# Hybrid DeltaNet and attention block: vector rows loaded on another queue, modulation pieces run in the middle of the groups, gate steps at other places

## The chip, the cores and the metric

The kernel runs on one core of a Trainium2 chip. The metric is the device time of one execution in microseconds. A time of a kernel is the median of its runs; beside it stands one execution taken by the profiler, from which all durations below come.

The engines have short names: PE is the matrix engine (PEld its weight loads), DVE the vector engine, ACT the scalar engine, POOL the general one, SP the engine that issues most of the loads. L12 is line 12 of the kernel. One clock column, PEclk, says at which share of full speed PE was allowed to run in a stretch.

## The reference, cut to what matters

One layer on 512 latent tokens (x) and 256 context tokens (ctx), both of width 2048, all in 32-bit floats:

```python
mod = jax.nn.silu(c) @ w_ada + b_ada            # w_ada: 2048 x 6144
shift, scale, gate = split(mod, 3)              # and the same for c_ctx: mod_c
h  = rms_norm(x,   norm_w) * (1 + scale)   + shift
hc = rms_norm(ctx, norm_w) * (1 + scale_c) + shift_c
... = split(h @ w_in), split(hc @ w_in)         # q, k, v of 8 DeltaNet heads, z, gates, q, k, v, z of attention
# DeltaNet heads: short convolution, normed q and k, decay gates, chunked scan in two directions
# attention heads: normed q and k, rotary positions, softmax over context and latent tokens
y = concat(gdn * silu(z), attn * silu(z_a)) @ w_out
return rms_norm(x + gate * y, final_norm_w)
```

The change touches the way to `h`, `hc` and the first head's projections, and the gates of the DeltaNet heads.

## The kernel before, in words

**Three passes.** Each product with `h` is made of three matmuls: the weights and `h` are split into a high and a low part (`whi_w`, `wlo_w`, `w0h`, `w0l`; `hh` and `hL`/`hC`, with L for the 512 latent and C for the 256 context columns), and high times high, high times low and low times high are added up.

**First stage, head.** SP loads a small table of constants (`cmain`), six blocks of 128 tokens (`xs`, 1 MB each: two of context, four of x), then the vector rows: `vrow` (c, c_ctx, b_ada, norm_w and the DeltaNet norm, as rows of 128) and `crow` (convolution taps) in six small DMAs. For each token block, `turn` squares it on ACT (`junk`) and transposes it on PE (`xt`, L314) into `xts`; `spread` makes the norm factors into a row for all partitions (`rp`, `rb`). After block 1, `vec_columns` transposes the vector rows (`pv`, L268), from which silu(c) (`cs`) comes.

**First stage, modulation.** `ada(g)` computes shift and scale for two of the 16 K tiles of 128: it loads four pieces of `w_ada` (`wada`, 1 MB in two DMAs, L352), multiplies each by `cs` (16 matmuls, L355), copies the sums (`part`, L360), transposes them (`adat`, L364) and adds them up to `md`. It is a generator: with `halves` it stops after its second piece, and always once more between `part` and `adat`. The six 1 MB buffers of the `xs` blocks are those of the pieces too. `make_h` then makes h of these two K tiles: `hf` on DVE (L395), its high part `hhL`/`hhC` on ACT (L397), and the low part on DVE (L403).

**First stage, groups.** A loop over eight groups of two K tiles runs the products of the first head. `project(k)` runs five tiles for K tile k: klat, klat1, qlat, vlat, qlat1, where klat, klat1 and vlat take the context columns as well. `slot` counts the ten tiles of a group, 0 to 9. At the slots in `steps` the loop runs the next part of `ada(g + 1)` after that tile, and after the last of them `make_h(g + 1)`. Where `steps` holds slot 10, which is never reached, the rest is done behind the loop of the group. `gate_sums(g)` (L411 and L413) multiplies `hf` by the 32 gate columns `wg`. `first_weights(k)` loads the weights of K tile k (`wraw_w` 256 KB, `w0r` 64 KB) with three buffers each, and splits them on ACT and POOL (`wlo_w`, L130). In the last group, `gates_in` is run in place of `ada`; its second step transposes the gate sums (`gtp`).

**Order.** In the first stage the code's order is PE's order. On the other engines a scheduler places the instructions, and the DMAs of SP's queue are issued in order; each waits for the DMA eight issues earlier and for its buffer.

**Second stage.** Here rows of projection matmuls are run as filler: `pull(n)` runs filler of n rows, `run(gen, n, ...)` alternates steps of a generator with it. `g1` is the generator of the gates of heads 1 to 7, in three steps: sums along the chunk (`gcp`, L555 and L559); exponentials on ACT up to `egl` (L561 to L566) with `gcum` on DVE (L560); a transpose (`gtr`, L570), with more behind it. `gdn_post_q(1)` is the convolution of q of head 1 (`cacc_q`, DVE L221), and `prep` the head's preparation, whose `tvh` and `pxa` follow.

Of the kernel before, what the change touches and what calls it, by code (L numbers as in the profile page):

```python
# [9 lines left out]
F32R = mybir.dt.float32r  # L10
# [58 lines left out]
def build(tc, a):  # L69
# [18 lines left out]
    NG = KT // 2  # L88
# [7 lines left out]
    def low_tile(m, g, dtype, nm):  # L96
        pool_, n, s = lows[m]
        return pool_.tile([128, 2, n], dtype, tag=f"l{s}{g}", bufs=1, name=f"{nm}{s}{g}")
# [185 lines left out]
    def big(shape, nm):  # L284
        return p0.tile(shape, F32, tag="big", bufs=BIG, name=nm)

    xss = []
    for t in range(6):
        xt_ = big([128, D], f"xs{t}")
        SY.dma_start(xt_, a["ctx"][0, t * 128:(t + 1) * 128] if t < 2 else a["x"][0, (t - 2) * 128:(t - 1) * 128])  # L290
        xss.append(xt_)
    SY.dma_start(vrow[64:80], a["c"].rearrange("b (k p) -> (b k) p", p=128))
    SY.dma_start(vrow[80:96], a["c_ctx"].rearrange("(k p) -> k p", p=128))
    SY.dma_start(vrow[0:48], a["b_ada"].rearrange("b (k p) -> (b k) p", p=128))
    SY.dma_start(vrow[48:64], a["norm_w"].rearrange("b (k p) -> (b k) p", p=128))
    SY.dma_start(vrow[96:97], a["gdn_norm_w"])
    SY.dma_start(crow, a["conv_w"][0].rearrange("j (t p) -> (j t) p", p=128))
    banks = [lambda nm: stile([128, 4, 128], nm, "k"), lambda nm: stile([128, 4, 128], nm, "s"),
             lambda nm: stile([128, 4, 128], nm, "o"), lambda nm: btile([128, 4, 128], nm)]
    ssx = p0.tile([128, 6], F32, name="ssx")  # L300
# [38 lines left out]
    def ada(g, halves=False):  # L339

        n, k0, rows = 2, 2 * g, 4
        md = mds[g] = p0.tile([128, 2, 2, 2], F32, tag="md", bufs=4, name=f"md{g}")

        def vec(v):
            return v[:, k0:k0 + n].unsqueeze(2).to_broadcast([128, n, 2])

        ada_ps = gtile([128, 512], f"ada{g}")
        for j in range(KT // rows):
            wt = big([128, rows, 2, 256], f"wada{g}_{j}")
            for s in range(2):  # L350
                src = w_ada[j * rows * 128:(j + 1) * rows * 128, s * D + k0 * 128:s * D + k0 * 128 + 256]
                SY.dma_start(wt[:, :, s], src.rearrange("(k p) c -> p k c", p=128))  # L352
            for r in range(rows):
                kk = j * rows + r
                T.matmul(ada_ps[32 * r:32 * r + 32], lhsT=cs[:, kk], rhs=wt[:, r].rearrange("p s c -> p (s c)"),  # L355
                         start=kk < 4, stop=kk >= KT - 4, skip_group_check=True)
            if j == 1 and halves:
                yield
        part = p0.tile([128, 512], F32, tag="part", bufs=2, name=f"part{g}")
        V.tensor_copy(part, ada_ps)  # L360
        yield
        tp = gtile([128, 4, 128], f"adat{g}")
        for i in range(4):
            T.transpose(out=tp[:, i], in_=part[:, i * 128:(i + 1) * 128], identity=ident)  # L364
        V.tensor_reduce(out=md.rearrange("p s i m -> p (s i) m"),
                        in_=tp.rearrange("p a (g m) -> p a m g", g=4)[:, :, 0:2], axis=AX.X, op=ALU.add)
        V.tensor_tensor(out=md[:, 0], in0=md[:, 0], in1=vec(vT), op=ALU.add)
        V.tensor_tensor(out=md[:, 1], in0=md[:, 1], in1=vec(b1), op=ALU.add)
        mul(V, md[:, 1], md[:, 1], vec(vT[:, 48:64]))
# [18 lines left out]
    def make_h(p_):  # L388

        md = mds[p_]  # L390
        for i in range(2):
            k = 2 * p_ + i
            hf = hfs[k] = p0.tile([128, NTOK], F32, tag="hf", bufs=3, name=f"hf{k}")
            for m_, t0, t1 in ((0, 0, SEQ), (1, SEQ, NTOK)):
                V.scalar_tensor_tensor(out=hf[:, t0:t1], in0=xts[m_, p_][:, i], scalar=md[:, 1, i, m_:m_ + 1],  # L395
                                       in1=rb[:, t0:t1], op0=ALU.mult, op1=ALU.mult)
                S.activation(hh[m_][:, k], hf[:, t0:t1], AF.Identity, bias=md[:, 0, i, m_:m_ + 1])  # L397
        for m_ in range(2):
            hls[m_, p_] = low_tile(m_, p_, F32R, "h")
        for i in range(2):  # L400
            k = 2 * p_ + i
            for m_, t0, t1 in ((0, 0, SEQ), (1, SEQ, NTOK)):
                V.scalar_tensor_tensor(out=hl(m_, k), in0=hfs[k][:, t0:t1], scalar=md[:, 0, i, m_:m_ + 1],  # L403
                                       in1=hh[m_][:, k], op0=ALU.add, op1=ALU.subtract)
# [34 lines left out]
    def gates_in():  # L439

        V.tensor_copy(gsh, gps[96:128, 0:2])
        for j in range(3):
            c0 = (j + 1) % 3 * 256
            V.tensor_scalar(out=gsb[:, c0:c0 + 256], in0=gps[32 * j:32 * j + 32], scalar1=gsh[:, j // 2:j // 2 + 1],
                            scalar2=None, op0=ALU.add)
        for lo_c, n in ((0, 4), (4, 8)):
            v = gsb[:, lo_c * 64:(lo_c + n) * 64].rearrange("p (c t) -> p c t", t=64)
            p_lo = 0 if n == 4 else 2
            V.tensor_copy(gso[:, p_lo:p_lo + n // 2, 0], v[:, 0:n // 2])
            V.tensor_copy(gso[:, p_lo:p_lo + n // 2, 1], v[:, n // 2:n][:, ::-1])  # L450
        yield
        gtp = gtile([128, 6, 32], "gtp")
        for p in range(6):
            T.transpose(out=gtp[:, p], in_=gso[:, p].rearrange("g h t -> g (h t)"), identity=ident[:32, :32])
        S.activation(adt[:, 0], adt[:, 0], AF.Exp)
        for hf_ in range(2):
            pr = slice(64 * hf_, 64 * hf_ + 64)
            for v in range(2):
                d = v if hf_ == 0 else 1 - v
                src = gtp[pr].rearrange("t p (k d h) -> t d k h p", k=2, d=2)[:, d]  # L460
                V.tensor_copy(gx[pr, :, :, v], src)
                s2 = adt[pr].rearrange("t k (d h) -> t d k h", d=2)[:, d].unsqueeze(3).to_broadcast([64, 2, 8, 6])
                V.tensor_copy(adv[pr, :, :, v], s2)
        S.activation(gsc["beta"], flat(gx[:, 0]), AF.Tanh, scale=0.5)
        V.tensor_scalar(out=gsc["beta"], in0=gsc["beta"], scalar1=0.5, scalar2=0.5, op0=ALU.mult, op1=ALU.add)
        V.tensor_tensor(out=zg, in0=flat(gx[:, 1]), in1=flat(adv[:, 1]), op=ALU.add)
        V.tensor_copy(ag, flat(adv[:, 0]))
        V.scalar_tensor_tensor(out=ug, in0=zg, scalar=-1.0, in1=zg, op0=ALU.mult, op1=ALU.min)
        S.activation(ug, ug, AF.Exp)
# [25 lines left out]
    gps = cctx1[:, 1]  # L495
    for g in range(NG):
        slot = 0
        ahead = ada(g + 1, g < 2) if g + 1 < NG else gates_in()
        steps = (5, 9, 10) if g < 2 else (6, 8) if g == 2 else (3, 5)
        for k in (2 * g, 2 * g + 1):  # L500
            if k + 2 < KT:
                first_weights(k + 2)
            if k == 8:
                SY.dma_start(ctri, a["ctri"])
                SY.dma_start(adt[:, 0], a["a_log"].rearrange("b d h -> b (d h)").to_broadcast([128, 16]))
                SY.dma_start(adt[:, 1], a["dt_bias"].rearrange("b d h -> b (d h)").to_broadcast([128, 16]))
            for _ in project(k):
                if slot == (0 if g + 1 == NG else steps[0]):
                    gate_sums(g)
                if g + 1 < NG:  # L510
                    if slot in steps:
                        next(ahead, None)
                        if slot == steps[-1]:
                            make_h(g + 1)
                elif slot == 1:
                    with tc.high_priority(offset=2500):
                        next(ahead)
                slot += 1
        if g < 2:
            next(ahead, None)  # L520
            make_h(g + 1)


    with tc.high_priority(offset=2500):
        next(ahead, None)
    es0.close()

    growd = dram.tile([2, 96, 64], F32, name="growd")
# [83 lines left out]
    def gdn_post_q(h, raw):  # L612
        kq = kq_of(h)
        acc, e, off = conv(h, f"q{h}", raw, False)
        x, y = [t[:, :SEQ].rearrange("p (c t) -> p c t", t=64) for t in (acc, e)]
        silu(V, kq[:, 0:4, 64:128], x[:, 0:4], y[:, 0:4])
        silu(V, kq[:, 4:8, 0:64], x[:, 4:8], y[:, 4:8])
# [539 lines left out]
    for i, n in enumerate((3000, 5500, 5500, 4000, 14000, 6000)):  # L1157
        pull(n)
        next(prep, None)
        if i == 4:  # L1160
            gdn_post_k(1, raws[3])
    gdn_post_q(1, raws[4])
    es_x.close()
    run(g1, 3000, 9000, 8000)
    es1.close()
    gp2 = es_g.enter_context(tc.tile_pool(name="gp2", bufs=1, reuse_waits="tile"))
    UUs.append(gp2.tile([128, 12, 128], F32, name="UU1"))
    zero(UUs[1].rearrange("p a d -> p (a d)"))
    run(prep, 5000, 30000, 5000, 7000, 6000)
    tail = None  # L1170
    for h in range(NH):
        while (h + 1 if h + 1 < NH else "kva") not in fed:
# [409 lines left out]
```

## Time and profile before

| what | value |
|---|---|
| median of 3 runs | 1390.62 us (1388.72 to 1392.34) |
| the profiled execution | 1388.62 us, span of its instructions 1386.8 us |
| PE busy | 1274.0 us, 92% of the span |
| DVE, ACT, POOL busy | 777.9, 585.3, 455.9 us |
| granted PE clock, mean | 0.972 |
| HBM traffic | 148.85 MB read, 14.08 MB written |

The profiled execution lies 2.00 us under the median of the runs. Its time is 1.8 us more than its span: what lies before the first and after the last instruction. PE is the busiest engine all through, so a wait on another engine counts only where PE waits for it in the end. The first 180 us are the first stage; this part differs from the rest in that the DMA engines are nearly full there, and that PE has gaps.

### The profile page before, as it was taken

To read this page: it belongs to the slowest core of one execution; us is meant where nothing else is said; L and a number is where in the kernel's file an instruction comes from. 1 tells how busy PE (TensorE), PEld (TensorE's weight loads), DVE (VectorE), ACT (ScalarE), POOL (GpSimd) and SP (SyncE) were. 2 spreads that over 40 slices of the span, in tenths; PEclk is the share of its full clock that TensorE was granted. 3 is DMA by queue.
4 is the path that set the end of the run, shared out by engine and by line. 5 is a ranking of instruction groups with operands and counts; after the bars stand their busy time and mean duration, and the time that the engine had idled before them with its cause. 6 is when DMAs were issued, how large, how long until landed. Compare 5 with 4: busy or idle time off the path is not lost. (4 is left out here: it accounts for less than half of the span.)

```text
span 1386.8 us, 24425 instructions
## 1 busy us (share of the span) xinstructions
PE 1274.0 (92%) x9226; PEld 1036.5 (75%) x9226; DVE 777.9 (56%) x1662; ACT 585.3 (42%) x1464; POOL 455.9 (33%) x437
## 2 busy tenths in 40 slices
PE   5789999999989999999889998999899999999997
PEld 4456677877778787877777786777788788777785
DVE  4325587486664658464665524315888787544322
ACT  4212263443535454454545434444454444433211
POOL 1212223344334433443433444453223232021330
PEclk9799999999999999999999999999999999999999
DMA  9979523232222323322232434347344334564212
GB/s 332 297 251 316 175 61 88 76 64 59 52 57 81 63 52 72 77 62 56 58 63 63 96 98 123 94 108 253 118 121 146 99 114 122 183 227 145 91 39 91
DMA packets 227002, 164.55 MB, mean 119 GB/s; under 512 B 62210, under 2 KB 198491, under 8 KB 225859
## 3 DMA queue, kind: packets, MB, share of 16 engines
q1 hardware_dynamic: 226883, 162.98, 40.3%
q8 instruction: 73, 1.20, 0.4%
q14 instruction: 46, 0.38, 0.1%
HBM read 148.85 MB, written 14.08 MB: 117 GB/s over the span
## 5 line engine op out<-in xcount | busy, mean ns | idle before, releaser
L130 POOL TENSOR_TENSOR wlo_z<-wraw_z,whi_z 128x512 fp32r<-128x512 f32 x44 | 67.2, 1542 | 140.9 <-ACT whi_z L129 122.2
L240 POOL TENSOR_TENSOR sdh<-sth,egl 128x256 f32<-128x256 f32 x80 | 55.0, 688 | 140.1 <-DVE sth L900 100.5
L874 DVE SCALAR_TENSOR_TENSOR rh<-ksh,negeg,vtokh 64x128 f32<-64x128 f32 x176 | 61.2, 348 | 53.4 <-PE ksh L862 45.3
L879 ACT ACTIVATE oqh<-ksh,egsw 64x128 f32<-64x128 f32 x128 | 46.4, 362 | 103.3 <-DVE rh L874 95.5
L147 PE MATMUL po<-wlo_wo,mh 128*128 128x512 f32 x192 | 77.5, 404 | 4.3 <-DVE wlo_wo L130 4.3
L146 PE MATMUL po<-whi_wo,mh 128*128 128x512 f32 x192 | 76.3, 400 | 1.2 <-ACT whi_wo L129 0.8
L148 PE MATMUL po<-whi_wo,ml 128*128 128x512 f32 x192 | 76.8, 400 | 0.0
L900 DVE TENSOR_TENSOR sth<-sdh,tsh 128x256 f32<-128x256 f32 x80 | 33.5, 419 | 76.4 <-PE tsh L894 67.7
L1363 PE MATMUL zl<-hhL,whi_z 128*128 128x512 f32 x176 | 74.1, 421 | 0.0
L130 DVE TENSOR_TENSOR wlo_wo<-wraw_wo,whi_wo 128x512 fp32r<-128x512 f32 x48 | 37.7, 793 | 64.0 <-ACT whi_wo L129 64.0
L1363 PE MATMUL zl<-hhL,wlo_z 128*128 128x512 f32 x176 | 69.8, 396 | 0.1
L1363 PE MATMUL zl<-hL,whi_z 128*128 128x512 f32 x176 | 69.5, 395 | 0.0
L894 PE MATMUL tsh<-vsh,ktok 128*128 128x128 f32 x352 | 57.3, 286 | 8.5 <-ACT vsh L887 5.6
L894 PEld LDWEIGHTS tsh<-vsh,ktok 128*128 128x128 f32 x352 | 48.7, 195 | 18.4 <-ACT vsh L887 8.8
L1404 DVE SCALAR_TENSOR_TENSOR gacc<-graw,scol,gacc 128x512 f32<-128x512 f32 x60 | 60.0, 1000 | 1.2
L1513 POOL TENSOR_TENSOR yx<-yx,tt 128x512 f32<-128x512 f32 x12 | 17.1, 1440 | 128.7 <-DVE tt L240 128.7
L130 POOL TENSOR_TENSOR wlo_v<-wraw_v,whi_v 128x512 fp32r<-128x512 f32 x28 | 39.1, 1395 | 57.8 <-ACT whi_v L129 57.7
L129 ACT CAST whi_wo<-wraw_wo 128x512 fp32r<-128x512 f32 x48 | 29.3, 618 | 65.0 <-PE po L148 47.9
L883 PE MATMUL tsh<-rh,UU 128*128 128x128 f32 x176 | 37.2, 294 | 18.1 <-DVE rh L874 18.0
L221 DVE SCALAR_TENSOR_TENSOR cacc_v<-craw,cvT,cacc_v 128x512 f32<-128x512 f32 (+1 forms) x64 | 45.2, 750 | 10.4 <-ACT cacc_v L217 10.1
L887 ACT ACTIVATE vsh<-tsh,cch 128x128 f32<-128x128 f32 x88 | 32.3, 367 | 43.6 <-PE tsh L883 42.3
L883 PEld LDWEIGHTS tsh<-rh,UU 128*128 128x128 f32 x176 | 29.1, 193 | 27.6 <-issue 20.1
(542 smaller groups left out, 4153.2 us busy)
## 6 DMA issues: line engine op xcount, KB each, us to landing
wada<-in_w_ada SPq DMA_DIRECT2D x64, 512.0 KB, 7.1
graw<-in_w_ada SPq DMA_DIRECT2D x64, 256.0 KB, 3.5
wraw_wo<-in_w_out SPq DMA_DIRECT2D x48, 256.0 KB, 2.9
wraw_z<-in_w_in SPq DMA_DIRECT2D x44, 256.0 KB, 3.3
wraw_v<-in_w_in SPq DMA_DIRECT2D x28, 256.0 KB, 2.9
wraw_k<-in_w_in SPq DMA_DIRECT2D x24, 256.0 KB, 2.9
wraw_q<-in_w_in SPq DMA_DIRECT2D x24, 256.0 KB, 3.0
xs<-in_x SPq DMA_DIRECT2D x4, 1024.0 KB
```

The costliest lines, as they stand in the source:

```text
L130: (lo_eng or G).tensor_tensor(out=lo, in0=raw, in1=hi, op=ALU.subtract)
L146: T.matmul(out, lhsT=lh, rhs=rh, start=start, stop=False, skip_group_check=True)
L147: T.matmul(out, lhsT=lh, rhs=rl, start=False, stop=False, skip_group_check=True)
L148: T.matmul(out, lhsT=ll, rhs=rh, start=False, stop=stop, skip_group_check=True)
L221: V.scalar_tensor_tensor(out=x, in0=raw[:, i0 + j:i0 + j + m], scalar=w(j), in1=x, op0=ALU.mult, op1=ALU.add)
L240: eng.tensor_tensor(out=out, in0=x, in1=y, op=ALU.mult)
L874: V.scalar_tensor_tensor(out=r[rows], in0=ks[rows, d], scalar=gsc["negeg"][rows, gcol:gcol + 1], in1=vtok[rows, p], op0=ALU.mult, op1=ALU.add)
L879: S.activation(oq[rows, v, p - 2], ks[rows, d], AF.Copy, scale=gsc["egsw"][rows, gcol:gcol + 1])
L883: T.matmul(ts[:, 2], lhsT=UU[:, w], rhs=r, start=True, stop=True, skip_group_check=True)
L894: T.matmul(ts[:, d], lhsT=ktok[:, p, half], rhs=vs, start=True, stop=True, skip_group_check=True)
L1363: T.matmul(pl, lhsT=lw, rhs=rt, start=k == 0 and m == 0, stop=k == KT - 1 and m == 2, skip_group_check=True)
L1404: V.scalar_tensor_tensor(out=acc, in0=raw, scalar=scol[:, k:k + 1], in1=acc, op0=ALU.mult, op1=ALU.add)
```

## The change

The six DMAs of the vector rows go from SP's queue to ACT's, ahead of the `xs` loads. `ada` runs in halves for the first three groups (two before), at other slots, none of them slot 10, so that `adat` and `make_h` stand inside the group. `gate_sums` moves behind that step of its slot. `make_h` makes the low part of a K tile before it goes to the next. The transposes `gtp` move ahead of the last tile of the last group. In the second stage, two steps of `g1` and the filler between them move ahead of `gdn_post_q(1)`; the filler behind them is divided differently, with the same total.

```diff
+    S.dma_start(vrow[64:80], ...c...)          # six DMAs, now on ACT's queue and ahead of xs
+    ...
     for t in range(6):
         xt_ = big([128, D], f"xs{t}")
         SY.dma_start(xt_, ...)
-    SY.dma_start(vrow[64:80], ...c...)         # the same six on SP's queue
-    ...
     def make_h(p_):
         md = mds[p_]
+        for m_ in range(2):
+            hls[m_, p_] = low_tile(m_, p_, F32R, "h")
         for i in range(2):
             ...                                # hf and hh of K tile k
-        for m_ in range(2):
-            hls[m_, p_] = low_tile(m_, p_, F32R, "h")
-        for i in range(2):
-            k = 2 * p_ + i
             for m_, t0, t1 in ((0, 0, SEQ), (1, SEQ, NTOK)):
                 V.scalar_tensor_tensor(out=hl(m_, k), ...)
     for g in range(NG):
-        ahead = ada(g + 1, g < 2) if g + 1 < NG else gates_in()
-        steps = (5, 9, 10) if g < 2 else (6, 8) if g == 2 else (3, 5)
+        ahead = ada(g + 1, g < 3) if g + 1 < NG else gates_in()
+        steps = ((3, 5, 6), (2, 5, 6), (2, 4, 5), (3, 5))[min(g, 3)]
+        sums = 0 if g + 1 == NG else steps[-1] if g < 2 else steps[0]
             for _ in project(k):
-                if slot == (0 if g + 1 == NG else steps[0]):
-                    gate_sums(g)
                 if g + 1 < NG:
                     ...                        # next(ahead), make_h(g + 1)
-                elif slot == 1:
+                elif slot in (1, 8):
                     with tc.high_priority(offset=2500):
-                        next(ahead)
+                        next(ahead, None)
+                if slot == sums:
+                    gate_sums(g)
                 slot += 1
-        if g < 2:
-            next(ahead, None)
-            make_h(g + 1)
-    with tc.high_priority(offset=2500):
-        next(ahead, None)
...
+    pull(3000)
+    next(g1)
+    pull(9000)
+    with first_of_all():
+        next(g1)
     gdn_post_q(1, raws[4])
     es_x.close()
-    run(g1, 3000, 9000, 8000)
+    run(g1, 14000)
...
-    run(prep, 5000, 30000, 5000, 7000, 6000)
+    run(prep, 5000, 24000, 5000, 7000, 6000)
```

PE in the second half of group 0, before. The names carry running numbers; `cctx_498<-hf` and `cctx_498<-md` are the gate sums, `ada_562` is the sum of `ada(1)`, `qlat_496` is the tile qlat1, and the last row is the first matmul of group 1:

```order
L411 MATMUL cctx_498<-hf_476,wg 32x256 x3
L413 MATMUL cctx_498<-md_370,wg 32x2
L411 MATMUL cctx_498<-hf_481,wg 32x256 x3
L413 MATMUL cctx_498<-md_370,wg 32x2
L355 MATMUL ada_562<-wada_0_563,cs 32x512 x4
L355 MATMUL ada_562<-wada_1_570,cs 32x512 x4
...
L424 MATMUL qlat_496<-hhL,wlo_w_1_466 128x512
L355 MATMUL ada_562<-wada_2_595,cs 32x512 x4
L355 MATMUL ada_562<-wada_3_602,cs 32x512 x4
L364 MATMUL adat_611<-cmain,part_609 128x128 x4
L424 MATMUL klat_492<-hhL,whi_w_2_501 128x512
```

Before, the second half and `adat` are the last that PE does in the group, with the next group's first tile right behind. PE at the same place after the change (the first half of `ada(1)` stands further up, ahead of qlat1 of the first K tile; `klat_495` is the tile klat1, `qlat_494` qlat):

```order
L355 MATMUL ada_533<-wada_2_569,cs 32x512 x4
L355 MATMUL ada_533<-wada_3_576,cs 32x512 x4
L422 MATMUL klat_495<-hhL,whi_w_1_465 128x512
...
L424 MATMUL cctx_498<-hhC,wlo_w_1_466 128x256
L364 MATMUL adat_591<-cmain,part_583 128x128 x4
L409 MATMUL cctx_498<-hf_478,wg 32x256 x3
L411 MATMUL cctx_498<-md_370,wg 32x2
L409 MATMUL cctx_498<-hf_485,wg 32x256 x3
L411 MATMUL cctx_498<-md_370,wg 32x2
L422 MATMUL qlat_494<-hhL,whi_w_1_465 128x512
```

The second half now stands one tile ahead of `adat`, and the gate sums and three tiles (qlat, vlat, qlat1) stand between `adat` and the next group.

SP's queue after the token blocks, before:

```order
L296 DMA vrow<-in_gdn_norm_w 1x128
L297 DMA crow<-in_conv_w 120x128
L352 DMA wada_0_372<-in_w_ada 128x4x256 x2
...
L381 DMA w0r_505<-in_w_in 128x128
L138 DMA wraw_w_3_535<-in_w_in 128x2x256
L381 DMA w0r_541<-in_w_in 128x128
L352 DMA wada_0_563<-in_w_ada 128x4x256 x2
L352 DMA wada_1_570<-in_w_ada 128x4x256 x2
L352 DMA wada_2_595<-in_w_ada 128x4x256 x2
```

and after:

```order
L296 DMA xs_149<-in_x 128x2048
L352 DMA wada_0_372<-in_w_ada 128x4x256 x2
...
L381 DMA w0r_505<-in_w_in 128x128
L352 DMA wada_0_534<-in_w_ada 128x4x256 x2
L352 DMA wada_1_541<-in_w_ada 128x4x256 x2
L138 DMA wraw_w_3_551<-in_w_in 128x2x256
L381 DMA w0r_557<-in_w_in 128x128
L352 DMA wada_2_569<-in_w_ada 128x4x256 x2
```

The rows of vectors are gone from it (ACT's queue starts with them), and the first two pieces of `ada(1)` are issued ahead of the weights of K tile 3.

In the built program the order on DVE of the parts of `make_h` is the same before and after (all four `hf`, then the low parts), and behind the first `tvh` that follows `gtr` PE's order is the same in both.

More of the change, by code (lines that the diff above doesn't have):

```diff
@@ L285, in big @@
         return p0.tile(shape, F32, tag="big", bufs=BIG, name=nm)
+    S.dma_start(vrow[64:80], a["c"].rearrange("b (k p) -> (b k) p", p=128))
+    S.dma_start(vrow[80:96], a["c_ctx"].rearrange("(k p) -> k p", p=128))
+    S.dma_start(vrow[0:48], a["b_ada"].rearrange("b (k p) -> (b k) p", p=128))
+    S.dma_start(vrow[48:64], a["norm_w"].rearrange("b (k p) -> (b k) p", p=128))
+    S.dma_start(vrow[96:97], a["gdn_norm_w"])
+    S.dma_start(crow, a["conv_w"][0].rearrange("j (t p) -> (j t) p", p=128))
     xss = []
@@ L291, in build @@
         xss.append(xt_)
[L292 to L297, printed above, removed]
     banks = [lambda nm: stile([128, 4, 128], nm, "k"), lambda nm: stile([128, 4, 128], nm, "s"),
```

## The prediction

> **What bounds the kernel now.** I read the page first: its span, the busy row of PE, and the span in slices (one digit for each 34.7 us: busy tenths of PE, the granted PE clock).
>
> ```profile
> span 1386.8 us, 24425 instructions
> PE 1274.0 (92%) x9226; PEld 1036.5 (75%) x9226; DVE 777.9 (56%) x1662; ACT 585.3 (42%) x1464; POOL 455.9 (33%) x437
> PE   5789999999989999999889998999899999999997
> PEclk9799999999999999999999999999999999999999
> ```
>
> PE bounds the kernel at 92%. Of what it leaves unused much stands in the first four slices (5, 7, 8, 9; one low clock digit). So I read that stage by its own parts: a table of stretches, each from the first klat matmul of a group to that of the next. Columns: length, busy time of PE, PEld, DVE, ACT, POOL, then clock, DMA share, GB/s.
>
> ```profile
> 42.72:65.13 22.41, 18.33 (x100) 11.84 (x100) 6.81 (x14) 4.57 (x11) 5.54 (x6) 0.80 1.08 344
> 65.13:86.16 21.03, 17.57 (x101) 11.50 (x101) 5.61 (x14) 4.02 (x9) 3.48 (x4) 0.86 1.03 330
> 86.16:104.92 18.76, 16.59 (x100) 11.06 (x100) 5.61 (x13) 3.96 (x8) 3.26 (x4) 0.91 0.58 189
> 104.92:122.94 18.02, 16.52 (x101) 11.25 (x101) 8.79 (x22) 4.48 (x10) 2.12 (x4) 0.91 0.93 303
> 122.94:137.54 14.60, 14.50 (x101) 9.84 (x100) 6.84 (x14) 3.77 (x9) 4.29 (x5) 1.00 1.03 329
> 137.54:152.19 14.65, 14.54 (x101) 9.85 (x100) 6.85 (x14) 3.77 (x9) 4.29 (x5) 1.00 1.03 325
> ```
>
> The same work takes 14.6 us in groups 4 and 5, at full clock and without gaps, and 22.4, 21.0, 18.8 and 18.0 us in groups 0 to 3. Why, the waits of PE up to 260 us tell (total, times, longest).
>
> ```profile
> PE klat L424 <- ACT hhL L397: 9.0, 4, 2.8
> PE pv L268 <- DMA vrow<-in_norm_w: 7.7, 1, 7.7
> PE gtr L570 <- ACT egl L566: 2.3, 1, 2.3
> PE kvl L164 <- ACT craw L201: 2.0, 1, 2.0
> ```
>
> The end of group 0 on PE's timeline (start, busy, what; in brackets the idle time before it and who ended it):
>
> ```profile
> 59.44 1.92 PE L355 MATMUL ada<-wada,cs 128*32 128x512 f32 x16
> 62.18 0.66 PE L364 MATMUL adat<-cmain,part 128*128 128x128 f32 x4 [0.81 <-DVE part L360]
> 65.13 0.79 PE L424 MATMUL klat<-hhL,whi_w 128*128 128x512 f32 x1 [2.29 <-ACT hhL L397]
> 66.49 0.80 PE L424 MATMUL klat<-hL,whi_w 128*128 128x512 f32 x1 [0.36 <-DVE hL L403]
> ```
>
> PE ends group 0 with the second half of ada(1), waits 0.81 for its copy, transposes, and then waits 2.29 us until h of the next group is made, with nothing queued that it could do. Such a gap costs twice, as the clock shows in stretches around two of them:
>
> ```profile
> 37.00:50.60 13.60, 8.99 (x30) 5.92 (x23) 7.29 (x13) 4.48 (x10) 5.42 (x6) 0.50 0.86 264
> 64.30:71.10 6.80, 5.61 (x15) 4.44 (x16) 3.59 (x8) 2.18 (x4) 0.00 (x0) 0.50 1.10 345
> 231.50:235.00 3.50, 3.50 (x15) 3.12 (x14) 3.33 (x8) 0.62 (x1) 2.27 (x2) 0.51 0.35 88
> ```
>
> After the gap that ended at 65.13 PE runs 5.9 us at half clock (to 71.10), in which a matmul takes twice as long: 2.9 us more. After the 2.3 us for `gtr` it is 3.5 us, so 1.75 more.
>
> **Groups 0 to 3.** The change puts the second half and `adat` of the first two groups inside the group, as groups 3 to 5 have it before. The evidence that this hides the chain of `part`, `adat`, `md`, `hf`, `hh` and `hL` is the rows of groups 4 and 5, whose successors' `adat` stands four tiles from the end: 0.1 us idle in 14.6. In groups 0 and 1 there will be three tiles and the gate sums. From the start of `adat` the chain needs 65.13 - 62.18 = 2.95 us to klat and 66.49 - 62.18 = 4.31 us to `hL`. What PE has there is priced by these rows of group 5:
>
> ```profile
> 137.54 0.40 PE L424 MATMUL klat<-hhL,whi_w 128*128 128x512 f32 x1
> 140.12 0.39 PE L424 MATMUL qlat<-hhL,whi_w 128*128 128x512 f32 x1
> 140.82 0.40 PE L424 MATMUL vlat<-hhL,w0h 128*128 128x512 f32 x1
> 141.97 0.42 PE L411 MATMUL cctx<-hf,wg 128*32 128x256 f32 x3
> 142.86 3.61 PE L355 MATMUL ada<-wada,cs 128*32 128x512 f32 x31
> ```
>
> A q tile is 140.82 - 140.12 = 0.70, the v tile 141.97 - 140.82 = 1.15, one of the two klat tiles (140.12 - 137.54) / 2 = 1.3, the gate sums 142.86 - 141.97 = 0.9, the transposes 0.66. To the next klat that is 0.66 + 0.9 + 0.70 + 1.15 + 0.70 = 4.1 us, over 2.95; the first matmul that takes `hL` comes 0.36 later, at 4.5, and `hL` is there at 4.31. The low part of the context half follows half a microsecond behind, so I allow 0.3 us for each of the two groups. Group 2 (`adat` ahead of four tiles, as in groups 3 to 5) and group 3 (its code is unchanged; its clock stretch came from the wait in front of it) go to 14.6. The copy `part` (0.81) is covered by the klat1 tile (1.3).
>
> Group 1: 21.03 - 14.6 - 0.3 = 6.1. Group 2: 18.76 - 14.6 = 4.2. Group 3: 18.02 - 14.6 = 3.4. Group 0 starts out of a gap (the head's last, below) and keeps its half-clock stretch, 50.60 - 42.72 = 7.9 us, which costs half, 3.9; with 0.8 for its first waits for `hL` and `hC` it takes 19.3, and 0.3 at its end: gain 22.41 - 19.6 = 2.8. Its bounds are 18.0 (two clock windows of about 3.4 us) and 20.5. Together 16.5 us.
>
> **Do the pieces come in time?** This carries the forecast, since in groups 0 and 1 the second pieces are now wanted some 6 us before the group's end, not at it. A group takes 4 pieces of 1.05 MB and two K tiles of weights of 0.33 MB, 4.85 MB. At the 344 GB/s of group 0 (DMA share 1.08, full) that is 14.1 us, at 330 it is 14.7: PE wants one group each 14.6. So the DMA engines become almost as tight as PE. SP is held by the buffers before (an SP wait row below), not by the rate, in groups 2 and 3 (189 and 303 GB/s). Here the first pieces of ada(1) are issued about 36 us (below); with 2 us until they flow, all of ada(1) and the weights between have landed at 37.5 + 14.1 = 51.6. PE wants the last pieces after three klat tiles, two q tiles, a v tile and a half of ada (2.0, as 31 of 32 matmuls take 3.61): 3.9 + 1.4 + 1.15 + 2.0 = 8.4 us at full clock, which from 40.3 on, with 7.9 us at half clock, is 52.6. Then each side adds its period: landing 65.7 against about 67.5 wanted, 79.7 against 82, 93.8 against 96. The margin is 1 to 2 us all the way; at 335 GB/s it is half of that. I take no loss from it and leave the shortfall to a rival.
>
> **Head.** The rows of SP, PE and the DMA table (vrow: KB, us to landing):
>
> ```profile
> vrow<-in_c SPq DMA_DIRECT2D x1, 8.0 KB, 15.1
> 4.45 0.47 SPq L292 DMA_DIRECT2D vrow<-in_c  x1
> 16.66 10.89 SPq L352 DMA_DIRECT2D wada<-in_w_ada  x8
> 31.82 6.00 SPq L138 DMA_DIRECT2D wraw_w<-in_w_in  x1
> 36.47 1.49 PE L355 MATMUL ada<-wada,cs 128*32 128x512 f32 x8 [2.12 <-DMA wada<-in_w_ada]
> 42.72 0.80 PE L424 MATMUL klat<-hhL,whi_w 128*128 128x512 f32 x1 [2.85 <-ACT hhL L397]
> SPq L352 <- PE ada L355: 37.8, 9, 12.9
> 17.50:21.00 3.50, 0.67 (x4) 0.70 (x5) 0.15 (x1) 2.69 (x3) 0.55 (x1) 0.50 0.80 238
> 20.00:36.30 16.30, 13.66 (x102) 10.64 (x102) 11.21 (x40) 4.56 (x13) 0.58 (x1) 0.90 0.94 283
> ```
>
> An 8 KB row issued at 4.45 lands at 19.6, behind the six token blocks, so PE stands 7.7 us; the first wada piece is issued behind the small rows, at 16.66. With six rows issued on ACT's queue in the first microseconds, `pv` finds them early, and wada can go out as soon as block 0 is transposed. The 7.7 us are not the gain: group 0 starts 6.25 us after the last pieces of ada(0), which PE waits for until 36.47, and this is a matter of DMA. 283 GB/s x 16.3 us = 4.6 MB land between 20.0 and 36.3. At 344 they take 13.4, so 2.9 us less at most (3.6 if the 238 GB/s before 20 fill up too). The fourth piece cannot go before block 3 is squared and transposed, at about 16.5, so I take 2.4 of it; the bound below is 0. The six issues cost ACT under 0.5 us each, before its first block is there. SP's 6.00 us on the weights of K tile 2 move up by the same 2.4, to end at 35.4, and the pieces of ada(1) go next, not behind the weights of K tile 3 as before (which wait for POOL).
>
> A rule of the Trainium skill speaks against this part: "DMA: Bandwidth & Descriptors", section "Issuing engines are not separate DMA queues", says that DMAs started by several engines run on the same 16 DMA engines and interleave, and that spreading them only saves the time to start them. By it the head gains some tenths of a microsecond for the issues, and the sum below would be 2 us less. No row here has a load on ACT's queue beside the blocks, so this trace cannot decide it.
>
> **Gates.** `gtp` ahead of the last tile: the 2.0 us of `kvl` wait for copies of the tiles and stay; the transposes go off the path, 0.3 us (bounds 0 and 2). For `gtr`:
>
> ```profile
> 222.95 0.98 PE L555 MATMUL gcp<-gg__116,ctri 128*128 128x42 f32 x8
> 224.25 0.51 PE L164 MATMUL kvl<-hhL,wlo_kv 128*128 128x512 f32 x1
> 229.25 0.23 DVE L560 COPY gcum<-gcp 128x84 f32<-128x84 f32 x1
> 230.40 0.24 ACT L566 ACTIVATE egl<-gcp 128x84 f32<-128x84 f32 x1
> 230.69 0.31 PE L570 MATMUL gtr<-cmain,gcum 128*84 128x128 f32 x1 [2.32 <-ACT egl L566]
> ```
>
> The filler between `gcp` and `gtr` was 230.69 - 2.32 - 224.25 = 4.1 us. By the built order it grows from 8448 to 13824 rows, so to 4.1 x 13824 / 8448 = 6.7 us: `gtr` is reached at 230.9, and `egl` is done at 230.64. The wait of 2.3 goes and with it the 1.75 of clock; 0.4 comes back at `pxa`, which has less filler in front of it. Sum 3.6, bounds 0 and 4.
>
> **Sum.** 16.5 + 2.4 + 0.3 + 3.6 = 22.8; less 0.6 for gaps on the way: 22.2. The profiled execution's own time is its span of 1386.8 and 1.8 around it, 1388.6, which gives 1366.4. The median of the runs shown, 1390.6, is 2.0 above that execution, and the forecast against it is 1368.4; I say 1368.
>
> **Rivals.** B, the pieces come late: what goes from PE's gap at a group's end returns as a wait in front of `ada` at slot 5. For it speaks the margin of 1 us, and the 325 to 330 GB/s of groups 1, 4 and 5; against it that PE did not wait for a piece there (no such row among its waits but the 2.12 below 40 us). At 320 GB/s a group takes 15.2 us, and over seven groups 4 us return; with two or three gaps of over 2 us and their half clock, 10. Time 1371 to 1378.
>
> C, slower: the same mechanism with the DMA engines as the bound. To lose, the seven groups would have to take 22.2 + 4.2 us more than 7 x 14.6 (102.2), 18.4 each: 264 GB/s. The first stage had 246 GB/s once in a long stretch (20 to 43 us, with SP held by buffers), but 344 and 330 where nothing held it. Time 1395.
>
> D, part of the change does nothing: the rows on ACT's queue land behind the blocks all the same, as the 8 KB of c did with 15.1 us, and PE waits as before; or `egl` stays late because DVE's convolution (ending at 229.2) is in front of `gcum`. 2.4 or 3.6 less: 1371 to 1372.
>
> E, the gaps go but the half-clock stretches stay, because they hang on something else than gaps of 2 us. "TensorE: Matmul & The Clock Gate" of the Trainium skill, Part 1, gives an idle window of about 3.4 us as what brings half clock back. By that rule the gaps of 2.3 us would not do it. This trace disagrees: 2.29 and 2.32 us of waiting stand in front of 64.30 and 231.50. Worked out from rows, what the clock takes in groups 1 to 3 (0.14 x 21.03, 0.09 x 18.76, 0.09 x 18.02) and at `gtr` is 2.9 + 1.7 + 1.6 + 1.75 = 8 us; if that stays the time is 1376.
>
> **How the numbers follow.** My forecast has 0.52 (its own range 1364 to 1371), B 0.22, D 0.14, E 0.04, C 0.03; 0.05 is left for more gain (group 0 at full clock earlier, the whole 3.6 at the head): 1361 to 1364. The range from 1362 to 1377 leaves out C, the upper end of B and the lowest cases. A measurement of this kernel tells 0.3% (4.2 us) from no change: every case but C and a heap of B and D lies under 1386. So faster 0.94, same 0.03, slower 0.03.
>
> **What would show it.** Groups 1 to 3 at 14.6 to 14.9 us each with clock 1.00, no row of klat waiting for `hhL` over 0.5 us but at group 0; `pv` without its 7.7; group 0 starting at 40.3; no `gtr` wait over 0.3. Wrong would be a row of `ada` waiting for wada over 1 us in groups 0 to 3 (B), `hL` rows over 0.8 per group (the cover of three tiles is too thin), or group 0 starting at 42.7 (D).

## The result and the profile after

The changed kernel takes 1374.14 us, median of four runs (1369.89 to 1376.49), against 1391.48 for the kernel before: a ratio of 0.9874, 95% interval 0.9844 to 0.9904, some 17 us less. Run again later (below) it gave 1370.76 and 0.987. The forecast was 1368, in a range of 1362 to 1377. The profiled execution took 1373.23 us; the forecast against its counterpart was 1366.4, so 6.8 us are to be explained.

The page, the same rows as shown of before:

```profile
span 1371.5 us, 24428 instructions
PE 1271.3 (93%) x9226; PEld 1032.2 (75%) x9226; DVE 781.6 (57%) x1662; ACT 583.7 (43%) x1464; POOL 458.2 (33%) x437
PE   6899998999899999999899998998999999999997
PEclk9999999999999999999999999999999999999998
```

PE's work is the same; the first slices rose from 5, 7, 8, 9 to 6, 8, 9, 9, and the clock's 7 there is gone. The stretches from one group's first klat matmul to the next (columns as before), for groups 0 to 5:

```profile
39.64:58.20 18.56, 18.18 (x100) 11.83 (x101) 7.82 (x16) 4.96 (x11) 4.26 (x5) 0.82 1.10 349
58.20:73.69 15.49, 15.33 (x102) 9.37 (x101) 6.84 (x14) 3.88 (x9) 4.01 (x5) 1.00 1.10 348
73.69:88.49 14.80, 14.77 (x101) 9.44 (x100) 6.70 (x14) 3.67 (x9) 3.97 (x5) 1.00 1.10 346
88.49:103.11 14.62, 14.52 (x102) 9.69 (x101) 6.87 (x18) 3.27 (x9) 3.89 (x4) 1.00 0.99 316
103.11:118.33 15.22, 14.69 (x102) 9.68 (x101) 7.46 (x15) 4.39 (x10) 4.72 (x5) 1.00 1.10 347
118.33:132.93 14.60, 14.50 (x101) 9.69 (x100) 6.83 (x14) 3.76 (x9) 4.28 (x5) 1.00 1.10 346
```

Groups 0 to 3 took 22.41, 21.03, 18.76 and 18.02 us and take 18.56, 15.49, 14.80 and 14.62. Clock 1.00 in groups 1 to 3 says that the half-clock stretches went with the gaps. DMA share 1.10 at 346 to 349 GB/s in groups 0 to 2, where groups 1 and 2 had 1.03 and 0.58 before, says that the transfers now run all the way. Then the waits of PE up to 260 us:

```profile
PE xt L314 <- DMA xs<-in_ctx: 7.2, 1, 7.2
PE tvh L751 <- DVE gts__117 L564: 3.8, 1, 3.8
PE klat L422 <- ACT hhL L399: 3.5, 1, 3.5
PE ada L355 <- DMA wada<-in_w_ada: 3.1, 3, 1.9
PE kvl L164 <- DVE craw L201: 1.5, 1, 1.5
PE gtr L562 <- ACT egl L558: 0.9, 1, 0.9
```

`pv` is gone from the list, klat waits for `hhL` once (head) and not four times. The three waits for `wada` stand in the head too, at 23 to 34 us. The second row is new: 3.8 us of `tvh` waiting for a copy `gts` on DVE, in the second stage. Where it stands shows PE's and DVE's timelines:

```profile
204.20 0.34 PE L551 MATMUL gcp<-gg__116,cmain 64*128 64x84 f32 x1
211.04 0.31 PE L562 MATMUL gtr<-cmain,gcum 128*84 128x128 f32 x1
217.59 1.12 PE L751 MATMUL tvh<-cmain,vv 128*128 128x128 f32 x4 [3.79 <-DVE gts__117 L564]
230.54 0.22 PE L771 MATMUL pxah<-DTh,grh 32*32 32x32 f32 x2
```

```profile
209.60 0.24 DVE L552 COPY gcum<-gcp 128x84 f32<-128x84 f32 x1
...
211.61 1.31 DVE L738 TENSOR_TENSOR tmh<-NEh 96x44 f32<-96x44 f32 x1
212.96 1.21 DVE L740 TENSOR_TENSOR NEh<-NEh,tmh 96x44 f32<-96x44 f32 x1
...
217.26 0.28 DVE L564 COPY gts__117<-gtr 84x128 f32<-84x128 f32 x1
```

`gtr` is done at 211.3, but in DVE's order 23 small operations, nearly all of the preparation (`tmh`, `NEh`), stand between `gcum` and its copy to `gts`, which runs at 217.26. Before, 12 stood there, and the copy ran at 233.02, 2.0 us after the end of `gtr` at 231.0. The next tile of the same PSUM bank, the `tvh` of four transposes, waits for it; a bank here is one buffer that `gcp`, `gtr` and this tile take in turn.

Set against before, kvl is 19.6 us earlier (180.01 to 160.40), the first pxa 18.2 (248.74 to 230.54), the first matmul of `zl` 14.5 (945.05 to 930.54), the end 15.4. So the first stage gained more than forecast (18.6), the stretch with the gate steps, from kvl to pxa, lost 1.4 where 3.6 was to come, and 2.8 went in a part where PE has the same order in both. A half-clock stretch of 3.4 us costs PE 1.7, and from kvl to pxa there are two of them before (180.3 to 183.8 and 231.5 to 235.0) and one in the change (217.4 to 220.8), so the 1.4 holds only for this pair of executions.

### The profile page after: what moved, and what is told of

Read it like the earlier page. It is cut to its first block, busy times and chain, and to the rows that moved or that the text cites. A ratio compares the mean times of both kernels' runs of the same rounds, so it can differ in the third digit from the quotient of the medians.

```text
span 1371.5 us, 24428 instructions
## 1 busy us (share of the span) xinstructions
PE 1271.3 (93%) x9226; PEld 1032.2 (75%) x9226; DVE 781.6 (57%) x1662; ACT 583.7 (43%) x1464; POOL 458.2 (33%) x437
## 5 line engine op out<-in xcount | busy, mean ns | idle before, releaser
L130 POOL TENSOR_TENSOR wlo_v<-wraw_v,whi_v 128x512 fp32r<-128x512 f32 x28 | 38.1, 1362 | 59.3 <-ACT whi_v L129 59.2
L221 DVE SCALAR_TENSOR_TENSOR cacc_v<-craw,cvT,cacc_v 128x512 f32<-128x512 f32 (+1 forms) x64 | 44.1, 734 | 10.5 <-ACT cacc_v L217 10.2
```

The costliest lines, as they stand in the source:

```text
L130: (lo_eng or G).tensor_tensor(out=lo, in0=raw, in1=hi, op=ALU.subtract)
L221: V.scalar_tensor_tensor(out=x, in0=raw[:, i0 + j:i0 + j + m], scalar=w(j), in1=x, op0=ALU.mult, op1=ALU.add)
```

## The experiments

| what | median us | ratio to before | 95% interval |
|---|---|---|---|
| the change | 1374.14 | 0.9874 | 0.9844 to 0.9904 |
| the change, again | 1370.76 | 0.9870 | 0.9851 to 0.9889 |
| groups alone | 1370.47 | 0.9883 | 0.9859 to 0.9907 |
| vector rows alone | 1384.57 | 0.9979 | 0.9963 to 0.9996 |
| second stage alone | 1389.05 | 1.0008 | 0.9989 to 1.0026 |
| without the second stage's move | 1369.25 | 0.9871 | 0.9852 to 0.9889 |
| vector rows first on SP's queue | 1374.15 | 0.9895 | 0.9880 to 0.9910 |
| copy behind gtr on ACT | 1368.72 | 0.9864 | 0.9848 to 0.9881 |
| the same, more filler ahead of pxa | 1370.22 | 0.9867 | 0.9842 to 0.9892 |
| gtr in another bank | 1366.85 | 0.9866 | 0.9840 to 0.9893 |
| gtr in another bank, second stage as before | 1366.00 | 0.9872 | 0.9844 to 0.9900 |

The medians belong to different sessions, with the kernel before at 1385.83 to 1391.48; across rows the ratios are compared. Two more kernels were run once each, under the profiler, and have no ratio.

### The parts alone

Groups alone: `steps`, the order of `gate_sums`, `make_h` and the slot of `gtp` as in the change, all else as before.

> The kernel before with only the first stage's groups changed (pieces in halves inside the group, gate sums and gate transposes moved); vector rows stay on SP's queue behind the blocks, second stage as before. Theory A (the groups carry the gain by themselves): group 0 starts at 42.7 as before, groups 0 to 3 take about 18.6, 15.5, 14.8 and 14.6, kvl starts some 16.5 us earlier than before (163.5), and the time is 15 to 17 us under the kernel before. Rival (without the earlier start the pieces come late): rows of ada waiting for wada in groups 0 to 2, 1 to 3 us each, and less than 12 us of gain.

Measured: 0.9883, 16 us, as theory A had it. Its profiled execution ran at a granted clock of 0.927, so its lengths are not compared; in it group 0 starts at 40.63, kvl at 164.10, and ada waits for wada once from group 0 on, 0.6 us. The rival falls.

Vector rows alone: the six DMAs on ACT's queue, all else as before.

> The kernel before with only the vector rows moved to ACT's queue ahead of the blocks. Theory A: pv loses its wait of 7.7 us, group 0 starts about 3 us earlier (39.6), later groups keep their lengths, and the time is 3 us less. Rival (the rule that spreading loads over engines saves only the issue time): under 1 us. Second rival: the 3 us at the head are lost again in groups 0 to 3, which wait at their ends for h anyway; kvl gains under 1.5 us.

Measured: 0.9979, so 2.9 us (0.6 to 5.1). Group 0 starts at 39.16 and kvl at 175.15, against 42.72 and 180.01; `pv` is not among the waits. But the start of group 0 varies from one execution to the next: with the rows on SP behind the blocks it was 42.72 (before), 40.27 (second stage alone) and 40.63 (groups alone), with them on ACT 38.6 to 40.2 in ten profiles. What the traces give to the rows is thus nearer 2 us than 3.6, and the interval of the time does not rule out the rival's "under 1 us".

Second stage alone:

```diff
+    pull(3000)
+    next(g1)
+    pull(9000)
+    with first_of_all():
+        next(g1)
     gdn_post_q(1, raws[4])
-    run(g1, 3000, 9000, 8000)
+    run(g1, 14000)
-    run(prep, 5000, 30000, 5000, 7000, 6000)
+    run(prep, 5000, 24000, 5000, 7000, 6000)
```

> The kernel before with only the second stage's move of the gate steps. Theory A (the copy behind gtr stands late in DVE's order wherever the first stage ends): tvh waits 3 to 4 us for the copy, gtr under 1.2 us, from kvl to pxa it takes 70 us (68.7 before), and the time is the same within 0.2%, 1 to 2 us slower if anything. Rival B (the late copy comes only with the earlier first stage): no tvh wait, pxa 65 us after kvl, 3 to 4 us faster than before.

PE's timeline of that kernel:

```profile
233.21 0.66 PE L759 MATMUL tvh<-cmain,vv 128*128 128x128 f32 x4 [3.08 <-DVE gts__117 L572]
```

No gain: 1.0008. The wait of `gtr` is gone and a wait of 3.08 for the copy is there, so the late copy belongs to the move itself, not to the earlier first stage. From kvl to pxa it took 67.85 us, not 70: no half-clock stretch followed the gap in this execution. Theory A holds in the waits and in the time, not in that length.

The change with the second stage put back:

> The changed kernel with the second stage put back as in the kernel before. Theory A (the move of the gate steps costs, since the copy behind gtr comes late in DVE's order): no wait of tvh for the copy, gtr waits 2.3 us again, and from the first kvl to the first pxa it takes 68.7 us as before, not 70.1: 1.4 us faster than the changed kernel. Rival B (the move gained 3.6 us as forecast, the loss lies elsewhere): 3 to 4 us slower than the changed kernel, pxa 73 us after kvl.

0.9871: the same as with the move, within the interval. `gtr` waits 2.3 us again, `tvh` only 0.3. From kvl (162.31) to pxa (229.90) it took 67.59 us, 2.5 less than in the change, more than theory A's 1.4: this execution has no half-clock stretch there at all (clock 1.00), although the wait of `gtr` is as long as before, where one followed it. Rival B, 3 to 4 us slower, falls.

### What the new wait is

```diff
-        V.tensor_copy(gts, gtr)
+        S.copy(gts, gtr)
```

PE's order stays the same to the row.

> The changed kernel with one copy (gtr to gts) done by ACT, not DVE; the order on PE and the rest of DVE are the same. Theory A (the copy's place in DVE's queue, behind a row of small operations, makes tvh wait 3.8 us): the wait goes, the half-clock stretch behind it (217.4 to 220.8) goes, pxa comes 66 us after kvl, limited by DTh, and the time is 4 to 5 us under the changed kernel. Rival B (tvh waits for something else that ends at the same time, the copy only being the last): the wait stays over 2 us with another name.

ACT's and PE's timelines of that kernel:

```profile
212.17 0.26 ACT L564 COPY gts__117<-gtr 84x128 f32<-84x128 f32 x1
```

```profile
211.30 0.31 PE L562 MATMUL gtr<-cmain,gcum 128*84 128x128 f32 x1
213.89 0.60 PE L751 MATMUL tvh<-cmain,vv 128*128 128x128 f32 x4
226.78 0.22 PE L771 MATMUL pxah<-DTh,grh 32*32 32x32 f32 x2 [1.39 <-DVE DTh L763]
```

The copy runs behind `gtr` and two casts of ACT, `tvh` waits for nothing, and kvl to pxa takes 65.97 us (70.14 in the change), where 1.39 us of `pxa` is the new limit. All as theory A had it in the stage. In the whole time it is a miss: 0.9864 against 0.9870 and 0.9874 is about a microsecond, not 4 to 5, with intervals that overlap.

Then `gtr` in another PSUM bank, the copy left on DVE; the order on PE, DVE and ACT is the same to the row:

```diff
-        gtr = gtile([n, 128], "gtr" + nm)
+        gtr = btile([n, 128], "gtr" + nm)
```

> The changed kernel with gtr in another PSUM bank than gcp and tvh; the order on PE, DVE and ACT is the same to the row, and the copy behind gtr stays late on DVE (at 217). Theory A (tvh waits for the copy only because gtr holds its bank, and gtr waits for egl only because gcp holds it): both waits go, pxa waits up to 1.4 us for DTh and comes 66 us after kvl, the time as with the copy on ACT, 1366 to 1370, ratio 0.985 to 0.987. Rival B (tvh needs the copy's result or another thing that DVE does at that time): tvh waits 3 to 4 us as before.

```profile
PE kvl L164 <- DVE craw L201: 1.5, 1, 1.5
PE t1h L640 <- DVE kq L237: 1.1, 1, 1.1
PE tsh L875 <- DVE UU L821: 0.9, 1, 0.9
PE pxah L771 <- DVE DTh L763: 0.9, 1, 0.9
```

These are its longest waits of PE from 155 to 260 us: neither `gtr` nor `tvh` is among them. The copy is still late on DVE; `tvh` follows 2.6 us after `gtr` all the same, and pxa comes 65.5 us after kvl. So it was the bank: `tvh` waits until the copy has read `gtr`. By the same rule `gtr` waits until `egl` has read `gcp`, which the next kernel tries. It has the second stage as before:

> The changed kernel with the second stage as in the kernel before, and gtr in another PSUM bank. Theory A: gtr no longer waits for egl but for gcum alone, which DVE copies 1.2 us before egl is done: 1.1 us of wait instead of 2.3; nothing else new; pxa 66 to 67 us after kvl; ratio 0.985 to 0.988. Rival B (egl is needed by itself): 2.3 us again.

`gtr` waits 0.5 us, for `gcum` on DVE, not 2.3 for `egl`; pxa comes 66.3 us after kvl. Theory A again, the wait even shorter than it said: both waits came from the shared bank. In the time (0.9872) nothing of it can be told from 0.9871.

More filler ahead of `pxa`, on top of the copy on ACT (`run(prep, 5000, 27000, 5000, 6000, 4000)` for `24000 ... 7000, 6000`):

> The changed kernel with the copy behind gtr on ACT, and 3000 rows of filler taken from the last two steps of prep to the one ahead of pxa. Theory A (pxa then waits 1.4 us for DTh, which more filler covers): the wait of pxah goes, tsh waits no more than 1 us longer, 0.5 to 1.4 us under the version with the copy on ACT alone, so a ratio to the kernel before of 0.985 to 0.986. Rival B (the later steps need their filler): pxb or tsh wait 1.4 us more and the time is the same.

0.9867: no gain that can be measured, so rival B in the time. In the trace `pxa` waits no more and `tsh` no longer than before (0.9), but `gtr` waited 0.9 in that execution; kvl to pxa is 65.86 us, against 65.97.

### The queue, the margin, the cover

Vector rows ahead of the blocks, on SP's own queue:

> The changed kernel with the six vector rows ahead of the blocks on SP's own queue, not on ACT's. Theory A (the order counts, another queue only saves the issue time): pv is early as well, the blocks are issued 2 to 3 us later (six issues of 0.3 to 0.5), group 0 starts at 41 to 42.5 instead of 39.6, and the time is 1.5 to 2.5 us above the changed kernel. Rival B (a queue of its own is what brings the rows past the blocks): the rows still land early here since they are first, so only a start at 42.7 or later, with pv waiting again, would speak for it.

```profile
1.18 0.42 SPq L287 DMA_DIRECT2D vrow<-in_c  x1
...
3.39 0.32 SPq L292 DMA_DIRECT2D crow<-in_conv_w  x1
3.76 0.87 SPq L296 DMA_DIRECT2D xs<-in_ctx  x2
```

The blocks go out 2.6 us later (3.76 for 1.18). `pv` does not wait here either, and the first `wada` is issued at 12.61, against 10.98 in the change and 16.66 before. A row lands 2.2 us after its issue here, 2.4 in the change, where it took 15.1 before. So being ahead is what makes the rows early. But group 0 starts at 40.98, no earlier than in two of the three kernels with the rows behind the blocks (40.27 and 40.63), and the ratio is 0.9895 against 0.9870 of the change: 3.5 us behind it, with intervals that just overlap, and no better than the groups alone (0.9883). So no run shows that the order by itself gains time; what ACT's queue adds can be put down to the issues, 2.6 us. That is what the page "DMA: Bandwidth & Descriptors" of the Trainium skill says in its section "Issuing engines are not separate DMA queues": starting DMAs from several engines only saves the time to start them. The trace agrees. The prediction had read the page as a reason to expect only some tenths of a microsecond, but six issues at 0.32 to 0.42 us, one behind the other, are not so little.

256 KB more to move per K tile (a copy of the same weights to DRAM, which nothing uses):

> The changed kernel with 256 KB more to move for each K tile (the same weights copied once more to DRAM, unused), 5.4 instead of 4.85 MB per group. Theory A (the pieces come with a margin of 1 to 2 us only, DMA being full at 347 GB/s): a group needs 15.5 us or more, ada waits for wada in most of groups 0 to 4, kvl comes 5 to 10 us later than 160.4. Rival B (the margin is large): no such waits and kvl under 162.

One execution, 1382.0 us. Its groups 0 and 4, and two of PE's waits, the second of them in group 4:

```profile
39.73:63.07 23.34, 19.15 (x101) 11.64 (x101) 7.82 (x16) 4.97 (x11) 4.24 (x5) 0.82 1.08 355
108.20:126.94 18.74, 16.26 (x101) 10.89 (x100) 7.72 (x16) 3.88 (x9) 4.24 (x5) 0.91 1.10 356
```

```profile
PE ada L355 <- DMA wada<-in_w_ada: 7.5, 7, 1.9
PE cctx L426 <- DVE hC L403: 2.4, 1, 2.4
```

kvl comes at 169.61, 9 us later, with 11% more bytes. Theory A's 15.5 us per group is a miss, and so are its waits in most groups: the transfers ran at up to 359 GB/s, and the groups other than 0 and 4 keep 14.8 to 15.2. In group 0, 4.8 us longer than in the change, `ada` waited 0.45, 1.50 and 1.89 us for pieces. The 3.5 us of group 4 are not a late piece: PE waited 2.4 for `hC`, and the clock fell after it; on DVE copies for the gates (`adv`, `ag`) had come between the parts of h. So late pieces are shown for about half of the 9 us.

The margin is thin without extra load as well. Nine profiled kernels have the change's groups and nothing more to move. In two of them, the change among them, PE waits for no piece from group 0 on; in the other seven it waits for a piece of `ada(1)` in group 0, 0.6 to 1.9 us, in the change again 0.85. In the worst, without the second stage's move, group 0 took 21.55 us. From the start of group 0 to kvl the nine took 120.4 to 123.5 us, the three kernels with the old groups 136.0 to 137.3. The forecast's rival B is thus what happens in most executions, in a small size.

`adat` later: slot 8 in group 0, 9 in group 1, 7 in group 2 (`steps` with 8, 9, 7 as last).

> The changed kernel with adat and make_h two, three and two tiles later: at slot 8 of group 0, slot 9 of group 1, slot 7 of group 2. Theory A (what stands behind adat on PE must reach 2.95 us to the next klat, or PE waits for the rest): klat waits 0.7 us for hhL at the end of group 0, 1.4 at the end of group 1, 0.4 at the end of group 2; and if a gap over about 1.5 us brings half clock back, a stretch stands behind the one of group 1 alone: 1.7 us more. kvl 3 to 6 us later than 160.4. Rival B (the cover is not what counts, h is made early enough anyway): no wait over 0.3 us at those places.

One execution, 1385.1 us, kvl at 170.87: 10.5 us later than in the change, where theory A had 3 to 6. The ends of the three groups on PE's timeline:

```profile
55.69 0.60 PE L364 MATMUL adat<-cmain,part 128*128 128x128 f32 x4
58.58 0.50 PE L422 MATMUL klat<-hhL,whi_w 128*128 128x512 f32 x1 [0.40 <-ACT hhL L399]
59.94 0.50 PE L422 MATMUL klat<-hL,whi_w 128*128 128x512 f32 x1 [0.58 <-DVE hL L401]
61.35 0.39 PE L424 MATMUL cctx<-hC,whi_w 128*128 128x256 f32 x1 [0.91 <-DVE hC L401]
...
75.60 0.60 PE L364 MATMUL adat<-cmain,part 128*128 128x128 f32 x4
79.46 0.49 PE L422 MATMUL klat<-hhL,whi_w 128*128 128x512 f32 x1 [2.27 <-ACT hhL L399]
...
95.94 0.50 PE L422 MATMUL klat<-hhL,whi_w 128*128 128x512 f32 x1 [0.54 <-ACT hhL L399]
```

The cover is what counts: 0.40, 2.27 and 0.54 us for the 0.7, 1.4 and 0.4 expected. With two tiles less behind `adat` in group 0 the waits for `hL` and `hC` add 1.5 us; theory A had left such waits out, behind groups 1 and 2 as well (0.58, and 0.78 with 0.91), and the half-clock stretches came elsewhere than it said (last section). In group 1 the chain took 3.9 us, not 2.95: one addition of `md` on DVE took 1.14 us instead of 0.16, beside an operation of POOL (last section). DVE's and POOL's timelines there:

```profile
76.46 1.14 DVE L367 TENSOR_TENSOR md<-md,vT 128x4 f32<-128x4 f32 x1
```

```profile
76.31 1.27 POOL L130 TENSOR_TENSOR wlo_w<-wraw_w,whi_w 128x512 fp32r<-128x512 f32 x1 [0.65 <-ACT whi_w L129]
```

### The change once more

> The changed kernel once more, unaltered, on this chip beside the others. Theory A (behind the first pxa nothing differs from before but the number of half-clock stretches, which changes from run to run): from the first pxa to the first zl it takes 694 to 700 us with 8 to 12 stretches of 3.4 us behind 260 us, 1.7 us per stretch; the tvh wait of 3.8 us is there again; median 1370 to 1374. Rival B (the change itself slows the later part): 699 to 701 again with 11 or more stretches.

From pxa to `zl`, in the kernel before, in the change and in the change again:

```profile
248.74:945.05 696.31, 647.01 (x5898) 541.74 (x5897) 384.14 (x951) 323.38 (x910) 286.57 (x281) 0.99 0.30 75
```

```profile
230.54:930.54 700.00, 649.03 (x5897) 542.96 (x5897) 385.74 (x951) 323.36 (x910) 286.30 (x281) 0.98 0.30 75
```

```profile
229.39:925.02 695.63, 643.65 (x5898) 538.62 (x5897) 384.45 (x951) 323.24 (x910) 285.66 (x281) 0.99 0.30 75
```

The same program takes 700.00 in one execution and 695.63 in another, at clock 0.98 and 0.99, and the kernel before lies between them. Rival B falls, so the 2.8 us in the later part were the execution's, not the change's. In the clock's record behind 260 us and before the kernel's end there are 9, 11 and 9 half-clock stretches of 3.4 us, 1.7 us each; from pxa to `zl` alone 6, 7 and 4. Over all profiled kernels that part took from 694.22 us, with 4 stretches, to 702.15, with 10. The stretches do not account for all of it: between the change and the kernel before one more stretch makes 1.7 of 3.7 us, and what the rest is stays open.

## Why the prediction was right, and where not

- **Groups 0 to 3**, forecast 16.5 us: right, in the mechanism too. Alone they gave 16 us; from the start of group 0 to kvl the profiled execution gained 16.5 (137.29 to 120.76). The evidence drawn from groups 4 and 5 held, and so did the cover of three tiles: no klat waits for `hhL` or `hL` from group 1 on. Group 0 took 18.56 for the 19.6 of the forecast, group 1 15.49 for 14.9, and group 4 15.22 for 14.6, which partly cancel.
- **Head**, forecast 2.4: right in size (2.9 alone, interval 0.6 to 5.1), in part by luck. Group 0 of the kernel before started at 42.72, the latest of three starts with the rows behind the blocks, so the single trace that it was worked out from made the head look worse than it mostly is. A piece of its working was missing: SP issued the last four blocks at 7.13, not at 2.11, since the issues of the blocks now wait 1.7 us for `cmain` and 3.5 for the first block (SP's waits), which fits DMAs eight issues earlier when the rows on ACT's queue are counted; group 0 started early enough all the same.
- **Pieces in time**, forecast no loss: right in the profiled execution, where no ada waits in the groups, but not in general. In seven of nine executions a piece was late by 0.6 to 1.9 us, in three of them by more than the 1 us that the prediction named as the sign of rival B. In the length up to kvl it cost up to some 2.5 us.
- **Rival E**, half clock that hangs on something else than the gaps: fell, with clock 1.00 in groups 1 to 3.
- **Gates, the step that failed**: "The wait of 2.3 goes and with it the 1.75 of clock; 0.4 comes back at `pxa`", 3.6 us. `gtr` came to wait 0.9, not under 0.3, which is a small miss. What failed is that I followed its inputs and not what comes behind it on its bank: the built order has 23 rows between `gcum` and the copy of `gtr` on DVE instead of 12, and `tvh` behind the copy. The change's 3.8 us took the place of 2.3. Alone and within the change the move gave nothing (1.0008; 0.9871 without it, 0.9870 and 0.9874 with it). That is most of the 4 us between the forecast ratio, 1368.4 / 1390.6 = 0.984, and 0.987. The 1.75 of clock was not sure either: without the second stage's move the same wait of 2.3 brought no half clock.
- **The rest of the profiled execution's miss**, 2.8 us behind pxa, differs from one execution of the same program to the next, in part by the number of half-clock stretches, which the prediction took as fixed. Runs of one kernel spread over up to 11 us, so a forecast from one profiled execution has that much blur.
- **The number**: 1374.14 lies in the stated range, but above the 1364 to 1371 of the forecast's own case, where only rivals had been expected. What took the time, the bank behind `gtr` and the later part's blur, was none of the rivals, so that the range held it is partly luck. Run again, the change gave 1370.76, inside the forecast's own case, in a session where the kernel before was 2.7 us lower.

## What to carry to other kernels

A chain that ends a loop body (last piece, reduce, next input) is covered by moving its start up by as many tiles as it is long; the steady iterations of the same loop show the length that the others can have. When a producer is moved, follow what reads its buffer too: which engine empties it, how far back in that engine's order, and who takes the buffer next. Where transfers are full all through, count the margin in microseconds before asking for pieces earlier.

## What the hardware showed that I had not expected

**The clock.** Gaps of PE bring half clock back, but not by their length alone. In the kernel with `adat` later, the windows around the ends of groups 0, 1 and 2 are (length, busy, and the clock in the column before the last two):

```profile
58.60:62.00 3.40, 1.91 (x7) 1.13 (x8) 3.40 (x6) 1.86 (x4) 1.50 (x1) 0.99 1.10 348
62.00:65.40 3.40, 3.40 (x14) 2.36 (x17) 0.36 (x1) 0.00 (x0) 0.00 (x0) 0.50 1.10 345
75.70:79.10 3.40, 1.49 (x21) 0.72 (x19) 2.76 (x7) 0.94 (x2) 1.27 (x1) 1.00 1.10 346
79.10:82.50 3.40, 2.46 (x11) 1.71 (x12) 3.12 (x6) 1.76 (x4) 0.00 (x0) 1.00 1.10 346
96.10:99.50 3.40, 1.72 (x7) 0.94 (x8) 3.40 (x6) 1.72 (x4) 1.71 (x1) 1.00 1.04 328
99.50:102.90 3.40, 3.40 (x12) 2.82 (x11) 0.42 (x2) 0.00 (x0) 0.00 (x0) 0.50 0.77 260
```

Three gaps of 0.40, 0.58 and 0.91 us at the end of group 0 were followed by 3.4 us at half clock, and so were 0.54, 0.78 and 0.91 at the end of group 2. One gap of 2.27 was not, though PE was less busy in the window around it (1.49 against 1.91 and 1.72). The wait of 3.08 for the copy in the second stage alone brought none, the 3.79 in the change did; the wait of 2.32 for `egl` brought one in the kernel before and none without the second stage's move. "TensorE: Matmul & The Clock Gate" of the Trainium skill, Part 1, names an idle window of about 3.4 us; the stretches do come in multiples of 3.4 us, but none of these gaps is that long except the 3.79. What decides it stays open.

**DVE beside POOL.** The two operations on DVE that took 1.31 and 1.21 us at 211.61 (above), where their neighbours take 0.2, ran while POOL split weights:

```profile
211.58 2.53 POOL L130 TENSOR_TENSOR wlo_v<-wraw_v,whi_v 128x512 fp32r<-128x512 f32 x2 [5.54 <-ACT whi_v L129]
```

They end with POOL's two operations, as the 1.14 us one does in the kernel with `adat` later. The kernel before shows it too: 1.17 us at 231.45 beside 1.33 of POOL at 231.23, and 1.18 at 233.95 beside 1.27 at 233.79. So a small DVE operation with two inputs can wait a whole POOL operation out, here 2.1 us of the copy's lateness. The Trainium skill's page "GPSIMD Engine Reference" lists in section 1, "Specifications", that POOL shares its memory interfaces with DVE where DVE takes two inputs from SBUF; the trace agrees. It was not tried by itself.
